# Seven-product FFN blocks: the first product copied by ScalarE into the bank in which its partner accumulates, and tails in another order

## The chip, the core and the metric

The kernel runs on one core of a Trainium2 chip. The metric is the device time of one execution in microseconds (us); less is better. Five engines work side by side, each through its own queue in order: TensorE (PE in the profile: matrix products and transposes, written to the banks of PSUM), VectorE (DVE), ScalarE (ACT), GpSimd (POOL) and SyncE (SP, which issues the weight loads). They wait for each other by semaphores.

## The reference

A decoder trunk of two layers on 256 tokens of width 1024, all in float32. Each layer is FFN, mixer, FFN, each with a layer norm behind it; the mixer is sparse attention in the first layer and a state-space scan (SSD) in the second. So there are four FFNs, and they are what the change touches:

```python
def swiglu_ffn(x, w_in, w_out):
    gate, up = jnp.split(x @ w_in, 2, axis=-1)
    return (jax.nn.silu(gate) * up) @ w_out

x = layer_norm(DEEPNORM_ALPHA * x + 0.5 * swiglu_ffn(x, ffn1_w_in[i], ffn1_w_out[i]), ln_g[i, 0], ln_b[i, 0])
```

with `D_FF = 2816`, that is 22 columns of 128 in the hidden layer.

## The kernel before

**Weights in two parts.** Every float32 weight tile (`raw`, 128 x 1024) is split into a high part `wh` (a cast by ScalarE, L321) and a low part `wl` (a subtraction by VectorE, L349), and every product is three matmuls: high by high, high by low, low by high (L528 to L530). `W.highs()` makes high parts ahead, `W.lows(keep)` makes the low parts that are still owed but for the last `keep`; `W.get(u)` makes what unit `u` still lacks. A raw tile is free for the next load when its last part is made.

**Order.** Nothing is scheduled by a tool. The instructions of every engine stand in the order in which the Python code issues them. In an FFN small pieces of work (GLUs, transposes) are put into `queue` by `later(f, d)`, to be issued `d` steps further on; each `step()` issues what is due (`items()`) and then makes weight parts (`W.pump`).

**An FFN** first does four hidden columns in the plain way (`wide`), two more singly (`one`), then 16 columns in four *seven-product blocks* (`seven`), in which two pairs of hidden columns (half-pairs `w` and `w + 1`) and the two token halves form a 2 x 2 block product with seven half products instead of eight. The sums of weights that it needs are made by VectorE (L288) or by accumulating DMAs that GpSimd issues (L261). Between the products stand pieces of the output product (`out()`, into the four `acc` banks). The last six output weights are the *tail*: token half 0 first, then half 1, with the layer norms of both halves.

In a block, `X` and `Y` are "pmm" banks, and `Z` is a "ptr" bank. The product A11 goes into X and is copied by ScalarE to SBUF (`p1`, L935), since X is needed for further sums. At the block's end A12 is made in Z, and VectorE adds: `nc.vector.tensor_add(p1, Z, p1)` (`c11`, L929). One step later comes the GLU on `p1`: SiLU by ScalarE (L773), then, a step later again, a multiplication by VectorE (L779).

When both token halves of a half-pair have their hidden values, `turn` transposes them on TensorE (L765) into a "ptr" bank; ScalarE casts the high part `hH` out of it (L766), and VectorE writes the low part `hL` (L767), which ends the use of the bank. This happens twice around a block's end: first for `w + 1` (tiles `c`, transposed ahead of the next block's first product) and then for `w` (tiles `c` and `h`, transposed behind the next block's second product). There are two "ptr" banks, handed out in turn.

**The tail** (`tail`) makes all the low parts that it can, then runs half 0, the layer norm of half 0 (L611 to L635), half 1, and, within half 1, the transposes of the new x of half 0 (`XT.fill(0)`, L546). The transposes of half 1 (`fill(1)`) come in the next stage.

Of the kernel before, what the change touches and what calls it, by code (L numbers as in the profile page):

```python
# [10 lines left out]
F32 = mybir.dt.float32  # L11
# [175 lines left out]
FILL = 2  # L187
# [220 lines left out]
def trunk_kernel(ctx: ExitStack, tc: tile.TileContext, widths, forms, x, ln_g, ln_b, wts, kvg, convp,  # L408
                 dt_bias, a_log, d_skip, norm_g, out):
    nc = tc.nc  # L410
# [37 lines left out]
    def pspare(n):  # L448
# [4 lines left out]
        a, b = divmod(spare[0] - 2, 2)  # L453
        return psum.tile([128, 512], F32, name=nm("psp"), tag=f"acc{a}{b}", bufs=1)

    def ptr():
        return psum.tile([128, 512], F32, name=nm("ptr"), tag="ptr", bufs=2)

    W = Weights(nc, f4, ring, wts, widths, forms, SLOTS, RAWS)

# [224 lines left out]
            c = slice(hf * 512, (hf + 1) * 512)  # L685
            mm3(acc[t][hf], lh, ll, H[:, c], L[:, c], first, last)

    def tail(acc, c, gb, ks, u, lhs, first, last, hook=None, early=0, ff=False):

        n = len(ks)
        nxt = None
        m = 0 if last else n - 3
        order = [[(i, hf) for a, b in ((0, n - 2), (n - 2, n)) for hf in range(2) for i in range(a, b)],
                 [(i, hf) for i in range(m) for hf in range(2)] + [(i, hf) for hf in range(2) for i in range(m, n)]]
        W.highs(8)
        W.lows()
        for t in range(2):
            for s, (i, hf) in enumerate(order[t]):  # L700
                if s == n and not t and hook:
                    hook()
                if s == n + FILL and t and not last:
                    nxt = XT(ff)
                    nxt.fill(0)
                H, L = W.get(u + i)
                if t and hf and last:
                    continue
                cs = slice(hf * 512, (hf + 1) * 512)
                mm3(acc[t][hf], *lhs(ks[i], t), H[:, cs], L[:, cs], first and i == 0, i == n - 1)  # L710
                if t and hf:
                    W.free(u + i)
                    if s < 2 * n - 2:
                        W.highs()
                        if s < n + FILL - early:
                            W.lows()
            rest = None
            if t and last:
                rest = pmm()[:, :256]
                for q, ps in enumerate((acc[t][1][:, :256], rest)):  # L720
                    ws = slice(512 + q * 256, 768 + q * 256)
                    for i, k in enumerate(ks):
                        H, L = W.get(u + i)
                        mm3(ps, *lhs(k, t), H[:, ws], L[:, ws], q == 1 and i == 0, i == n - 1)
            if t:
                W.lows(len(W.late) - 2)
            layernorm(t, acc[t], c, gb, last, rest, (lambda: W.lows(len(W.late) - 1)) if t and not last else None)
            if not t:
                W.highs(8)
                W.lows()  # L730
        return nxt

    def ffn(xT, u0, ln_i, first=False, last=False, ff=False):
# [9 lines left out]
        def later(f, d=1):  # L743

            while len(queue) < d:
                queue.append([])
            queue[d - 1].append(f)

        def items():
            for f in queue.pop(0) if queue else []:  # L750
# [18 lines left out]
        def glu(t, w, c, sil=None):  # L769


            g, h = (c[:, :256], c[:, 256:]) if sil is None else (sil, f1("h"))
            nc.scalar.activation(g, c[:, :256], AF.Silu)  # L773
            out_of = sil is not None and (w >= WIDE or (t and w and not first))
            if out_of:
                nc.scalar.copy(h, c[:, 256:])

            def mul():
                nc.vector.tensor_mul(h, h if out_of else c[:, 256:], g)  # L779
                W.owe(800)  # L780
                ready.setdefault(w, {})[t] = h
                if len(ready[w]) == 2:
                    later(lambda: later(turn(w, ready.pop(w))), 2)

            later(mul)

# [85 lines left out]
        def one(j):  # L872

            nonlocal u
            bank = pmm if j % 2 == 0 else ptr
            if j % 2 == 0:
                hH[j // 2], hL[j // 2] = r2("hH"), r2("hL")
            H, L = [a[j // 2][:, (j % 2) * 256:(j % 2 + 1) * 256] for a in (hH, hL)]
# [1 line left out]

            def half(o):
                nonlocal u
                ps = bank()
                proj_w(ps, xT, u)
                W.product()
                u += 1
# [16 lines left out]
        def seven(j, outs):  # L903
# [7 lines left out]
            w = j // 2  # L911
            for i in (w, w + 1):
                hH[i], hL[i] = r2("hH"), r2("hL")
            X, Y, Z = pmm(), pmm(), None
            c1, c2 = f4("c1"), f4("c2")
            p1, u2, u3, y5 = c1[:, :512], c1[:, 512:], c2[:, :512], c2[:, 512:]

            def c12():
                nc.vector.tensor_sub(u2, Y, u2)
# [5 lines left out]
                W.owe(600)  # L925
                later(lambda: glu(1, w + 1, y5))

            def c11():
                nc.vector.tensor_add(p1, Z, p1)  # L929
                W.owe(600)  # L930
                later(lambda: glu(0, w, p1))

            product(X, "A11", True)
            product(Y, "Q1", True)
            nc.scalar.copy(p1, X)  # L935
            nc.scalar.copy(y5, Y)
            step(4, most=-1)
            out()
# [8 lines left out]
            nc.scalar.copy(u3, X)  # L947
            later(c22)
            step(most=-1)
            Z = ptr()  # L950
            product(Z, "A12", True)
            later(c11)
            step(most=-1)
            out()
            product(X, "A22", False)
            glu(1, w, X, f1("sil"))
            step(most=-1)
            out()

        steps, ks = ffn_plan()  # L960
        for kind, j, outs in steps:
            W.raws = 9 if j < 18 else 7
            if kind == 'S':
                seven(j, outs)
            else:
                one(j)
                out_pieces(outs)
        while queue:
            items()
        gb = load_ln(ln_i)  # L970
        if first:
            load_consts()
        return u + len(ks), tail(acc, 0.5, gb, ks, u, lhs, False, last, ff=ff)

    def attention(xT, u, ln_i):
        kiT = f1("kiT")
# [771 lines left out]
```

## Time and profile before

| | |
|---|---|
| median of 3 runs | 1022.22 us (1021.9 to 1022.5) |
| profiled execution | 1022.91 us, span 1021.2 us |
| TensorE busy | 1003.4 us (98%), granted clock 0.999 |
| VectorE busy | 906.6 us (89%) |
| ScalarE busy | 660.9 us (65%) |
| GpSimd busy | 111.7 us (11%) |
| DMA | 231.70 MB, mean 227 GB/s |

The busy time of an engine is the time in which it executes an instruction; waiting is not in it. In rows of the timeline the first number is the start in us from the span's start, the second the duration of the (merged) instructions, then engine, line, operation, the tile written and those read, the shapes, the count, and in brackets the idle time of the engine ahead of it with what ended it. Instructions of one engine overlap a little: the next one starts somewhat before the end of the one ahead, so a queue's pace is read from start to start. A view of waits gives: who waited for whom, the sum in us, how many times, the longest.

### The profile page before, as it was taken

The page shows a single profiled execution, that of the slowest core. Times are in us where ns is not written, and L with a number is a line of the kernel's source. Part 1 is how long each engine was busy: PE and PEld are TensorE (multiplying, and loading weights), DVE is VectorE, ACT ScalarE, POOL GpSimd, SP SyncE. Part 2 cuts the span into 40 slices and gives each one's busy share as a digit, 9 for nine tenths or more (in the row PEclk, how much of TensorE's full clock was granted, in tenths as well). Part 3 has the DMA queues.
Part 4 walks back from the last instruction along what each step waited for, and adds up shares of the span by engine and source line. Part 5 has one row for each costly group of instructions (what it writes and reads, how often), then busy time and mean ns, then how long its engine had stood idle before and what let it go on. Part 6 is the DMA issues. An engine that isn't in the chain of part 4 may idle for free.

```text
span 1021.2 us, 14610 instructions
## 1 busy us (share of the span) xinstructions
PE 1003.4 (98%) x5279; PEld 848.4 (83%) x5279; DVE 906.6 (89%) x1264; ACT 660.9 (65%) x965; POOL 111.7 (11%) x161
## 2 busy tenths in 40 slices
PE   9999999999999999999999999999999999999996
PEld 7888888888788888887888888899898888888885
DVE  6899999789788999998899999788989978899996
ACT  6676876476655767764576775486876645676670
POOL 0010110100010101101010110150111101010101
PEclk9999999999999999999999999999999999999999
DMA  9699999452554899894499999467765654699971
GB/s 366 197 289 285 243 254 355 150 172 76 203 184 128 270 277 246 257 388 170 125 272 278 243 261 355 162 179 236 208 210 173 239 201 132 168 263 288 284 247 41
DMA packets 65336, 231.70 MB, mean 227 GB/s; under 512 B 8032, under 2 KB 8032, under 8 KB 65264
## 3 DMA queue, kind: packets, MB, share of 16 engines
q1 hardware_dynamic: 53856, 189.84, 50.8%
q0 software_dynamic: 11120, 40.41, 21.6%
q8 instruction: 41, 0.67, 0.3%
q10 hardware_dynamic: 288, 0.52, 0.1%
q14 instruction: 31, 0.25, 0.1%
HBM read 193.48 MB, written 1.08 MB: 191 GB/s over the span
## 4 chain that ended last, share of the span: by engine, by line
PE 86%; DVE 8%; DMA 3%; issue 1%; ACT 1%; POOL 1%; POOLq 0%; DVEq 0%
PE pmm L530 13%; PE pmm L528 13%; PE pmm L529 13%; PE acc L528 8%; PE acc L530 8%; PE acc L529 8%; DVE wl L349 3%; PE ptr L530 2%; PE ptr L529 2%; PE ptr L528 2%; PE pxs L528 2%; PE pxs L530 2%; PE pxs L529 2%; PE pmm L677 1%; PE ptr L677 1%; DMA raw<-in_wts_dram 1%
## 5 line engine op out<-in xcount | busy, mean ns | idle before, releaser
L349 DVE TENSOR_TENSOR wl<-raw,wh 128x1024 fp32r<-128x1024 f32 (+2 forms) x423 | 494.8, 1213 | 14.1 <-ACT wh L321 13.9
L321 ACT CAST wh<-raw 128x1024 fp32r<-128x1024 f32 (+3 forms) x430 | 428.1, 1044 | 90.8 <-DVE raw L288 48.7
L529 PE MATMUL acc<-wl,hH 128*128 128x512 f32 (+1 forms) x352 | 136.8, 389 | 1.6 <-DVE wl L349 1.6
L528 PE MATMUL acc<-wh,hH 128*128 128x512 f32 (+1 forms) x352 | 138.1, 392 | 0.0
L530 PE MATMUL acc<-wh,hL 128*128 128x512 f32 (+1 forms) x352 | 136.6, 388 | 0.0
L528 PE MATMUL pmm<-wh,xT 128*128 128x512 f32 (+2 forms) x320 | 126.0, 394 | 0.0
L530 PE MATMUL pmm<-wh,xT 128*128 128x512 f32 (+2 forms) x320 | 123.4, 386 | 0.4 <-DVE xT L525 0.2
L529 PE MATMUL pmm<-wl,xT 128*128 128x512 f32 (+2 forms) x320 | 122.8, 384 | 0.0
L261 POOL DMA_DIRECT2D raw<-raw x64 | 55.7, 876 | 489.4 <-DVE raw L288 256.6
L530 PE MATMUL pmm<-wh,xf 128*128 128x512 f32 x256 | 99.6, 389 | 0.0
L528 PE MATMUL pmm<-wh,xf 128*128 128x512 f32 x256 | 99.6, 389 | 0.0
L529 PE MATMUL pmm<-wl,xf 128*128 128x512 f32 x256 | 99.6, 389 | 0.0
L529 PEld LDWEIGHTS acc<-wl,hH 128*128 128x128 f32 x352 | 66.2, 188 | 16.2 <-DVE wl L349 3.3
L530 PEld LDWEIGHTS acc<-wh,hL 128*128 128x128 f32 x352 | 66.1, 188 | 13.5
L288 DVE TENSOR_TENSOR raw<-raw,raw 128x1024 f32<-128x1024 f32 x64 | 77.0, 1218 | 0.2
L528 PEld LDWEIGHTS acc<-wh,hH 128*128 128x128 f32 x352 | 66.1, 188 | 13.0
L530 PEld LDWEIGHTS pmm<-wh,xT 128*128 128x128 f32 x320 | 60.1, 188 | 13.8 <-DVE xT L525 1.7
L529 PEld LDWEIGHTS pmm<-wl,xT 128*128 128x128 f32 x320 | 60.4, 189 | 10.9 <-DVE wl L349 0.3
L528 PEld LDWEIGHTS pmm<-wh,xT 128*128 128x128 f32 x320 | 60.3, 188 | 10.5
L528 PEld LDWEIGHTS pmm<-wh,xf 128*128 128x128 f32 x256 | 48.0, 188 | 10.0
L529 PEld LDWEIGHTS pmm<-wl,xf 128*128 128x128 f32 x256 | 48.0, 188 | 10.0
L530 PEld LDWEIGHTS pmm<-wh,xf 128*128 128x128 f32 x256 | 48.0, 188 | 9.9
(307 smaller groups left out, 1768.4 us busy)
## 6 DMA issues: line engine op xcount, KB each, us to landing
raw<-in_wts_dram SPq DMA_DIRECT2D x339, 512.0 KB, 5.9
raw<-raw POOLq DMA_DIRECT2D x64, 512.0 KB, 5.5
M<-scr POOLq DMA_DIRECT2D x8, 512.0 KB, 5.9
lng<-in_ln_g_dram SPq DMA_DIRECT2D x6, 512.0 KB, 5.3
lnb<-in_ln_b_dram SPq DMA_DIRECT2D x6, 512.0 KB, 5.9
wl<-raw POOLq DMA_DIRECT2D x5, 512.0 KB, 5.5
raw<-in_wts_dram SPq DMA_DIRECT2D x4, 408.0 KB, 5.0
out_dram<-x SPq DMA_DIRECT2D x4, 256.0 KB, 2.0
```

The source lines that it names most:

```text
L261: self.nc.gpsimd.dma_start(self.raw[r], self.raw[other], accum_op=ALU.add)
L288: self.nc.vector.tensor_add(self.raw[r], self.raw[r], self.raw[other])
L321: nc.scalar.copy(h[:, c:c + n], raw[:, c:c + n])
L349: self.nc.vector.tensor_sub(lo[:, s], raw[:, s], h[:, s].bitcast(F32))
L528: nc.tensor.matmul(ps, lh, rh, start=first, stop=False, skip_group_check=on)
L529: nc.tensor.matmul(ps, lh, rl, start=False, stop=False, skip_group_check=on)
L530: nc.tensor.matmul(ps, ll, rh, start=False, stop=last, skip_group_check=on)
L677: nc.tensor.matmul(ps, H[:, k * 128:(k + 1) * 128], xT.HL[:, k, :], start=k == 0, stop=False)
```

## The change

1. In a block, `Z` is taken at the start, and ScalarE copies A11 into it (`nc.scalar.copy(Z, X)`) instead of into SBUF. A12 is then accumulated onto it by TensorE (its first matmul no longer clears the bank). VectorE's addition `c11` is gone, and the GLU is issued at once behind A12, reading from the bank: SiLU and a copy of the second half by ScalarE, and the multiplication by VectorE at the next step.
2. `ptr()` names its two banks: they are handed out in turn, but as long as a block holds one for `Z`, every other call gets the other one. Both transposes around a block's end fall into that time.
3. `turn`'s second part (hL) is put ahead of what is queued for the next step (`soon`), instead of behind it.
4. In the tails of the FFNs (`own=True`), up to two low parts that belong to the next stage are left for later; those made within half 1 too; and one low part is made ahead of the last `items()`.

```diff
+    bank, held = [0], [None]
+
     def ptr():
-        return psum.tile([128, 512], F32, name=nm("ptr"), tag="ptr", bufs=2)
+        bank[0] = 1 - bank[0] if held[0] is None else 1 - held[0]
+        return psum.tile([128, 512], F32, name=nm("ptr"), tag=f"ptr{bank[0]}", bufs=1)
...
         W.highs(8)
-        W.lows()
+        W.lows(min(2, sum(v >= u + n for v in W.late)) if own else 0)
...
                     nxt.fill(0)
+                    if own:
+                        W.lows(1)
...
-                        if s < n + FILL - early:
+                        if s < n + FILL - early and not own:
                             W.lows()
...
+        def soon(f):
+            if not queue:
+                queue.append([])
+            queue[0].insert(0, f)
...
-                    later(lambda: later(turn(w, ready.pop(w))), 2)
+                    later(lambda: soon(turn(w, ready.pop(w))), 2)
...
-            X, Y, Z = pmm(), pmm(), None
+            X, Y, Z = pmm(), pmm(), ptr()
+            held[0] = bank[0]
...
-            def c11():
-                nc.vector.tensor_add(p1, Z, p1)
-                W.owe(600)
-                later(lambda: glu(0, w, p1))
-
             product(X, "A11", True)
             product(Y, "Q1", True)
-            nc.scalar.copy(p1, X)
+            nc.scalar.copy(Z, X)
...
-            Z = ptr()
-            product(Z, "A12", True)
-            later(c11)
+            product(Z, "A12", False)
+            glu(0, w, Z, f1("sil"))
             step(most=-1)
             out()
             product(X, "A22", False)
             glu(1, w, X, f1("sil"))
             step(most=-1)
             out()
+            held[0] = None
...
+        W.lows(1)
         while queue:
             items()
...
-        return u + len(ks), tail(acc, 0.5, gb, ks, u, lhs, False, last, ff=ff)
+        return u + len(ks), tail(acc, 0.5, gb, ks, u, lhs, False, last, ff=ff, own=True)
```

How instructions move: TensorE's are the same ones in the same order. On VectorE, at the end of the second block of the second FFN, before (`c_472` is the tile of `p1`, `c_473` that of `y5`, `ptr_3793` is Z, `raw` in L288 are sums of weights):

```order
L349 TENSOR_TENSOR wl_3767<-raw_3415,wh_3766 128x1024
L929 TENSOR_TENSOR c_472_3623<-ptr_3793,c_472_3623 128x512
L349 TENSOR_TENSOR wl_3788<-raw_3436,wh_3787 128x1024
L349 TENSOR_TENSOR wl_3791<-raw_3691,wh_3790 128x1024
L779 TENSOR_TENSOR c_473_3624<-c_473_3624 128x256
L349 TENSOR_TENSOR wl_3815<-raw_3693,wh_3814 128x1024
L349 TENSOR_TENSOR wl_3818<-raw_3713,wh_3817 128x1024
L288 TENSOR_TENSOR raw_3693<-raw_3693,raw_3737 128x1024
L288 TENSOR_TENSOR raw_3713<-raw_3713,raw_3739 128x1024
L779 TENSOR_TENSOR c_472_3623<-c_472_3623 128x256
L779 TENSOR_TENSOR h_3856<-h_3856,sil_3855 128x256
```

And after (all lines of the program's later part are numbered some 3 to 10 higher; L789 is the multiplication, `h_3817` and `sil_3816` are the GLU of Z):

```order
L349 TENSOR_TENSOR wl_3778<-raw_3424,wh_3777 128x1024
L789 TENSOR_TENSOR h_3817<-h_3817,sil_3816 128x256
L349 TENSOR_TENSOR wl_3799<-raw_3445,wh_3798 128x1024
L349 TENSOR_TENSOR wl_3802<-raw_3702,wh_3801 128x1024
L789 TENSOR_TENSOR c_484_3635<-c_484_3635 128x256
L349 TENSOR_TENSOR wl_3829<-raw_3704,wh_3828 128x1024
L349 TENSOR_TENSOR wl_3832<-raw_3724,wh_3831 128x1024
L288 TENSOR_TENSOR raw_3704<-raw_3704,raw_3748 128x1024
L288 TENSOR_TENSOR raw_3724<-raw_3724,raw_3750 128x1024
L789 TENSOR_TENSOR h_3869<-h_3869,sil_3868 128x256
```

The addition is gone, and the multiplication that stood behind both L288 now stands where the addition was. On ScalarE at the same place, before:

```order
L947 COPY c_473_3624<-pmm_3621 128x512
L321 CAST wh_3787<-raw_3436 128x1024
L321 CAST wh_3790<-raw_3691 128x1024
L773 ACTIVATE c_473_3624<-c_473_3624 128x256
L321 CAST wh_3814<-raw_3693 128x1024
L321 CAST wh_3817<-raw_3713 128x1024
L773 ACTIVATE c_472_3623<-c_472_3623 128x256
```

And after:

```order
L953 COPY c_484_3635<-pmm_3631 128x512
L321 CAST wh_3798<-raw_3445 128x1024
L321 CAST wh_3801<-raw_3702 128x1024
L783 ACTIVATE sil_3816<-ptr_3633 128x256
L786 COPY h_3817<-ptr_3633 128x256
L783 ACTIVATE c_484_3635<-c_484_3635 128x256
L321 CAST wh_3828<-raw_3704 128x1024
L321 CAST wh_3831<-raw_3724 128x1024
```

The SiLU of this half moved ahead by two casts, and a copy out of the bank came with it. On VectorE in the tail of the second FFN, from the last multiplication to the layer norm of half 0, before:

```order
L779 TENSOR_TENSOR h_4406<-h_4406,sil_4405 128x256
L349 TENSOR_TENSOR wl_4391<-raw_4312,wh_4390 128x1024
L767 TENSOR_TENSOR hL_4174<-ptr_4432,hH_4173 128x512
L767 TENSOR_TENSOR hL_4172<-ptr_4438,hH_4171 128x512
L349 TENSOR_TENSOR wl_4415<-raw_4314,wh_4414 128x1024
L349 TENSOR_TENSOR wl_4418<-raw_4335,wh_4417 128x1024
L349 TENSOR_TENSOR wl_4451<-raw_4360,wh_4450 128x1024
L349 TENSOR_TENSOR wl_4454<-raw_4362,wh_4453 128x1024
L349 TENSOR_TENSOR wl_4457<-raw_4386,wh_4456 128x1024
L349 TENSOR_TENSOR wl_4460<-raw_4388,wh_4459 128x1024
L349 TENSOR_TENSOR wl_4463<-raw_4412,wh_4462 128x1024
L611 SCALAR_TENSOR_TENSOR x_71<-acc_3392,x_71 128x512
```

And after:

```order
L789 TENSOR_TENSOR h_4423<-h_4423,sil_4422 128x256
L349 TENSOR_TENSOR wl_4408<-raw_4327,wh_4407 128x1024
L349 TENSOR_TENSOR wl_4431<-raw_4329,wh_4430 128x1024
L777 TENSOR_TENSOR hL_4188<-ptr_4451,hH_4187 128x512
L777 TENSOR_TENSOR hL_4186<-ptr_4458,hH_4185 128x512
L349 TENSOR_TENSOR wl_4434<-raw_4350,wh_4433 128x1024
L349 TENSOR_TENSOR wl_4470<-raw_4378,wh_4469 128x1024
L349 TENSOR_TENSOR wl_4473<-raw_4380,wh_4472 128x1024
L349 TENSOR_TENSOR wl_4476<-raw_4403,wh_4475 128x1024
L614 SCALAR_TENSOR_TENSOR x_71<-acc_3401,x_71 128x512
```

One low part moved ahead of the two hL, and two of the seven behind them now stand behind the layer norm of half 0 (ahead of the transposed x's low parts).

More of the change, by code (lines that the diff above doesn't have):

```diff
@@ L686, in out_k, with tail @@
             mm3(acc[t][hf], lh, ll, H[:, c], L[:, c], first, last)
-    def tail(acc, c, gb, ks, u, lhs, first, last, hook=None, early=0, ff=False):
+    def tail(acc, c, gb, ks, u, lhs, first, last, hook=None, early=0, ff=False, own=False):
         n = len(ks)
@@ L874, in one @@
             nonlocal u
-            bank = pmm if j % 2 == 0 else ptr
+            half_bank = pmm if j % 2 == 0 else ptr
             if j % 2 == 0:
@@ L882, in half @@
                 nonlocal u
-                ps = bank()
+                ps = half_bank()
                 proj_w(ps, xT, u)
@@ L913, in seven @@
                 hH[i], hL[i] = r2("hH"), r2("hL")
-            X, Y, Z = pmm(), pmm(), None
+            X, Y, Z = pmm(), pmm(), ptr()
+            held[0] = bank[0]
             c1, c2 = f4("c1"), f4("c2")
-            p1, u2, u3, y5 = c1[:, :512], c1[:, 512:], c2[:, :512], c2[:, 512:]
+            u2, u3, y5 = c1[:, 512:], c2[:, :512], c2[:, 512:]
             def c12():
```

## Prediction

> **What bounds the kernel now.** I read the page first: the busy times, then the chain that ended last.
>
> ```profile
> PE 1003.4 (98%) x5279; PEld 848.4 (83%) x5279; DVE 906.6 (89%) x1264; ACT 660.9 (65%) x965; POOL 111.7 (11%) x161
> PE 86%; DVE 8%; DMA 3%; issue 1%; ACT 1%; POOL 1%; POOLq 0%; DVEq 0%
> ```
>
> TensorE is busy for 1003.4 of 1021.2 us and is 86% of the chain. VectorE is off the path but has little room of its own: 89% over the whole span. The change leaves TensorE's instructions and their order as they are, so all it can do is add or take away waits of TensorE. The view of waits, for TensorE, shows those that VectorE causes:
>
> ```profile
> PE acc L529 <- DVE wl L349: 1.6, 4, 0.4
> PE pxT L546 <- DVE x L635: 1.3, 3, 0.8
> PE ptr L546 <- DVE x L635: 1.1, 2, 0.8
> PE pmm L530 <- DVE xT L525: 0.2, 1, 0.2
> ```
>
> Columns: sum in us, times, longest. Nearly all of these 4.2 us lie in the FFN tails (the last six output weights, then the layer norm of half 0). No row names a transpose L765 or a product of a seven-product block: inside the blocks TensorE waits for nothing. So at most about 4 us can be won, and only in the tails; in the blocks there are only waits to be added.
>
> **The removed addition, and what stands in its place.** This is VectorE, then ScalarE, then TensorE in the timeline, around the end of the second block of the second FFN and the start of its third block:
>
> ```profile
> 375.50 1.22 DVE L349 TENSOR_TENSOR wl<-raw,wh 128x1024 fp32r<-128x1024 f32 x1
> 376.95 0.69 DVE L929 TENSOR_TENSOR c<-ptr,c 128x512 f32<-128x512 f32 x1 [0.23 <-PE ptr L530]
> 377.56 2.35 DVE L349 TENSOR_TENSOR wl<-raw,wh 128x1024 fp32r<-128x1024 f32 x2
> ...
> 382.44 2.35 DVE L288 TENSOR_TENSOR raw<-raw,raw 128x1024 f32<-128x1024 f32 x2
> 384.71 0.42 DVE L779 TENSOR_TENSOR c<-c 128x256 f32<-128x256 f32 x1
> 385.37 0.43 DVE L779 TENSOR_TENSOR h<-h,sil 128x256 f32<-128x256 f32 x1 [0.24 <-ACT h L776]
> 385.71 3.49 DVE L349 TENSOR_TENSOR wl<-raw,wh 128x1024 fp32r<-128x1024 f32 x3
> 389.12 1.22 DVE L288 TENSOR_TENSOR raw<-raw,raw 128x1024 f32<-128x1024 f32 x1
> 390.26 0.68 DVE L767 TENSOR_TENSOR hL<-ptr,hH 128x512 fp32r<-128x512 f32 x1
> ```
>
> ```profile
> 374.23 0.59 ACT L947 COPY c<-pmm 128x512 f32<-128x512 f32 x1 [1.70 <-PE pmm L530]
> 375.83 2.00 ACT L321 CAST wh<-raw 128x1024 fp32r<-128x1024 f32 x2 [1.01 <-DMA raw<-raw]
> 377.74 0.41 ACT L773 ACTIVATE c<-c 128x256 f32<-128x256 f32 x1
> 383.74 1.06 ACT L321 CAST wh<-raw 128x1024 fp32r<-128x1024 f32 x1 [3.39 <-DVE raw L288]
> 384.70 0.37 ACT L773 ACTIVATE sil<-pmm 128x256 f32<-128x256 f32 x1
> 384.98 0.36 ACT L776 COPY h<-pmm 128x256 f32<-128x256 f32 x1
> 391.05 0.59 ACT L936 COPY c<-pmm 128x512 f32<-128x512 f32 x1 [1.90 <-PE pmm L530]
> ```
>
> ```profile
> 390.62 0.39 PE L530 MATMUL pmm<-wh,xf 128*128 128x512 f32 x1
> 390.85 0.38 PE L765 MATMUL ptr<-ident,c 128*128 128x128 f32 x2
> ```
>
> Before, VectorE waits 0.23 us for the product A12 and adds (0.61 us from start to next start). After, its next instruction there is the GLU's multiplication, which needs a SiLU and a copy by ScalarE out of the bank, and these stand in ScalarE's queue behind two weight casts. The second cast of a block's last sum waits for a DMA accumulation (idle 1.01 here, "DMA raw<-raw"). So after: SiLU at 377.74 (where the old SiLU started); multiplication 0.67 later, as from 384.70 to 385.37, at 378.41; VectorE free 0.34 later (385.37 to 385.71), at 378.75. Before it was free at 377.56. VectorE is late by d = 1.19 us, though it has one instruction less. In general d is ScalarE's idle time before that cast plus 0.18, and not less than 0.40, since SiLU, copy and multiplication (0.67 + 0.34) take the place of an addition of 0.61 even where ScalarE waits only for the product.
>
> Does VectorE catch up? The multiplication that no longer stands at 384.71 saves 0.34, but the next one waits for ScalarE (0.24 idle), whose cast at 383.74 waits for the first L288. That chain moves by d as a whole. From 385.71 VectorE has no gap up to the write of hL at 390.26, so hL ends at 390.94 + d.
>
> **The bank.** Who needs that hL in time? Before, the two transposes of a block's ends (first of half-pair w+1, then of w) use the two "ptr" banks in turn, and nobody waits. After, Z holds one bank from the block's start to its end, and both transposes share the other: the second, at 390.85 in TensorE's order, must wait until VectorE has read the first, that is until hL is written. Before, the transpose starts 0.09 us ahead of that end. A release by VectorE takes 0.06 to TensorE (below: L635 ends at 461.57 + 0.75 = 462.32, transpose at 462.38). So TensorE waits d + 0.15, at three boundaries in each of four FFNs, 12 in all. (The fourth block's transposes fall behind the last block, where the banks are no longer held.) The shares of the idle time over all blocks:
>
> ```profile
> ACT wh L321 <- DMA raw<-raw: 11.5, 16, 1.3
> DVE c L919 <- ACT c L942: 13.5, 16, 1.1
> ```
>
> The first row gives 11.5 / 16 = 0.72 us a block, so d is 0.90 on average (1.48 at most, 0.40 at least). The second says that VectorE waits some 0.8 us for TensorE at L919 in every block: there the two fall into step again, so the delay doesn't pile up; but as TensorE was delayed 0.15 more than VectorE, the DMA accumulations of the next block start 0.15 early, and only the first boundary of each FFN pays the 0.15. Sum: 12 x 0.90 + 4 x 0.15 = 11.4 us. Bounds: 12 x 0.55 = 6.6 (every d at its least) and 12 x 1.63 = 19.6 (every d at its most).
>
> **Smaller parts of the blocks.** ScalarE's copy of the first product now goes into a bank; no row shows ScalarE writing a bank. The nearest row is the copy into SBUF beside it (0.59 at 391.05); as 1.90 us of idle follow before that one, waiting for TensorE, anything from nothing to 2.4 us for it is hidden, and I take nothing. The 16 extra ScalarE instructions (0.25 us each) fall into gaps of 1 to 3 us. The multiplication at 384.71 changes its place only.
>
> **The tails.** Here VectorE gets one low part ahead of the two hL (into the idle time behind the last multiplication) and two behind the layer norm of half 0 instead of ahead of it. From the second FFN's tail:
>
> ```profile
> 457.08 0.68 DVE L611 SCALAR_TENSOR_TENSOR x<-acc,x 128x512 f32<-128x512 f32 x1
> 461.57 0.75 DVE L635 SCALAR_TENSOR_TENSOR x<-x,rs,lnb 128x512 f32<-128x512 f32 x1 [0.73 <-POOL rs L520]
> 463.69 3.49 DVE L349 TENSOR_TENSOR wl<-raw,wh 128x1024 fp32r<-128x1024 f32 x3
> 469.43 0.68 DVE L611 SCALAR_TENSOR_TENSOR x<-acc,x 128x512 f32<-128x512 f32 x1
> 475.36 0.75 DVE L635 SCALAR_TENSOR_TENSOR x<-x,rs,lnb 128x512 f32<-128x512 f32 x1
> ```
>
> ```profile
> 462.38 0.66 PE L546 MATMUL pxT<-ident,x 128*128 128x128 f32 x4 [0.34 <-DVE x L635]
> 463.83 0.66 PE L546 MATMUL pxT<-ident,x 128*128 128x128 f32 x4 [0.79 <-DVE x L635]
> 476.36 1.03 PE L546 MATMUL pxT<-ident,x 128*128 128x128 f32 x8
> ```
>
> Three low parts of 1.14 us (3.49 / 3) leave the stretch ahead of 457.08, so the layer norm of half 0 can start up to 3.4 us earlier, as soon as its accumulator is done. The four waits of acc L529 (1.6 us) and those for half 0 go away. What is late next: the layer norm of half 1. Two low parts more stand ahead of it (2.3 us), so it starts at about 469.2 instead of 469.43, and its x is done at 475.36 + 0.75 = 476.1, where the second four of the transposes at 476.36 (at about 476.8) need it. TensorE can come only 0.7 + 0.2 = 0.9 us earlier there, not the 1.7 that its waits give. Likewise 0.7 in the first FFN; 0.7 in the third and 0.4 in the last, where the waits themselves are the limit. Together 2.7 us; between 1.6 (the waits for wl alone) and 4.2.
>
> **Sum.** 1022.9 us (the profiled execution, 1.7 above its span) + 11.4 - 2.7 = 1031.6. The median of the runs before lies 0.7 below the profiled one, so I forecast 1030.9 us, slower by 0.8%. About 0.2% (2 us) is what a measurement of this kernel can tell from no change.
>
> **The rivals.**
> 1. Tails and additions decide: hL comes in time. For it: hL was written only 0.09 us after the transpose starts. It takes a d below about 0.08 at every boundary (12 x (d + 0.15) less than 2.7), which means that ScalarE finishes SiLU and copy by the time at which the old addition ended. Against it: 0.67 + 0.34 stand against 0.61 even with no DMA wait. Time: 1022.2 - 2.7 = 1019.5, with all of the tails' waits 1018.0. Chance 0.06.
> 2. VectorE's instructions are on the path after all, and each addition taken away is time won: 16 x 0.61 = 9.8 us, so 1012.4. Against it: TensorE waits for VectorE 4.2 us in all, and none of it at the additions. Chance 0.01. The Trainium skill speaks for this one: "VectorE: DVE Perf Modes", section Rules for kernel authors, advises to cut the number of VectorE instructions. By that rule the count alone would tell; the trace agrees that an instruction of 512 columns costs 0.61 us of VectorE, and disagrees that VectorE sets the end.
> 3. About even: every d at its least (the accumulations land earlier because TensorE leaves them more time) and the tails win all: 1022.2 + 6.6 - 4.2 = 1024.6, or somewhat better, since a first boundary needs no more than 0.55. Within 0.2%: 0.08; between that and 1027 is part of my own case.
> 4. The lateness feeds itself: the accumulations that ScalarE waits for are issued by GpSimd after VectorE's low parts, so if their landing moves by more than the delay (they share the rings with twelve weight loads a block), d goes to its most: 1022.2 + 19.6 - 2.7 = 1039. Against it: they fall into step at L919. Chance 0.10.
> 5. My forecast, 1026 to 1035: 0.75.
>
> So faster 0.07, same 0.08, slower 0.85. The range 1022.5 to 1036.0 takes in most of 3 and the lower part of what lies between 5 and 4.
>
> **What would show it.** Right: a new row of TensorE's waits, ptr L775 on hL L777, 12 times, about 1 us each; VectorE's multiplication L789 at the block's end idle 1 to 2 us ahead of it, for ScalarE; the addition gone; the acc L532 waits gone; waits at L549 fewer but not gone (half 1 late). Wrong: no such row, or d below 0.3 because the weight casts stand earlier than I read, or waits for low parts (acc or pmm L532 on wl) in the blocks' middle, which would mean that VectorE's delay is not taken up at L919.

## The result, and the profile after

| | before | after |
|---|---|---|
| median | 1022.06 us (4 runs, 1021.61 to 1022.50) | 1029.99 us (4 runs, 1029.21 to 1030.94) |
| profiled execution, span | 1022.91 us, 1021.2 us | 1029.21 us, 1027.4 us |
| TensorE, VectorE busy | 1003.4, 906.6 us | 1005.1, 897.7 us |

The change makes the kernel slower: ratio 1.0074, 95% interval 1.0061 to 1.0086. Ratios and intervals, here and below, leave out four slow executions (1247, 2541 and 2835 us in two of the experiments, 1681 us of the kernel before), which the medians take in. VectorE has 8.9 us less to do, and the end comes 7.9 us later. TensorE's waits for VectorE in the profile after (sum in us, times, longest):

```profile
PE ptr L775 <- DVE hL L777: 5.9, 12, 1.0
PE ptr L549 <- DVE x L638: 2.2, 3, 0.9
PE pxT L549 <- DVE x L638: 1.7, 3, 0.8
PE pmm L532 <- DVE wl L349: 0.2, 1, 0.2
```

The first row is new, and it has the 12 waits of the forecast, at 0.5 us each where about 1 was forecast. The four waits of acc for wl are gone; those for x are still there, three and three instead of three and two. One of the 12 places, the end of the second block of the second FFN (the place of the prediction's rows), is this in VectorE's, ScalarE's and TensorE's timeline after:

```profile
378.97 1.22 DVE L349 TENSOR_TENSOR wl<-raw,wh 128x1024 fp32r<-128x1024 f32 x1
381.11 0.42 DVE L789 TENSOR_TENSOR h<-h,sil 128x256 f32<-128x256 f32 x1 [0.92 <-ACT h L786]
381.45 2.35 DVE L349 TENSOR_TENSOR wl<-raw,wh 128x1024 fp32r<-128x1024 f32 x2
...
389.26 0.43 DVE L789 TENSOR_TENSOR h<-h,sil 128x256 f32<-128x256 f32 x1 [0.58 <-ACT h L786]
389.60 3.49 DVE L349 TENSOR_TENSOR wl<-raw,wh 128x1024 fp32r<-128x1024 f32 x3
393.01 1.22 DVE L288 TENSOR_TENSOR raw<-raw,raw 128x1024 f32<-128x1024 f32 x1
394.15 0.69 DVE L777 TENSOR_TENSOR hL<-ptr,hH 128x512 fp32r<-128x512 f32 x1
```

```profile
377.71 0.59 ACT L953 COPY c<-pmm 128x512 f32<-128x512 f32 x1 [1.69 <-PE pmm L533]
378.19 2.00 ACT L321 CAST wh<-raw 128x1024 fp32r<-128x1024 f32 x2
380.43 0.38 ACT L783 ACTIVATE sil<-ptr 128x256 f32<-128x256 f32 x1 [0.23 <-PE ptr L533]
380.71 0.37 ACT L786 COPY h<-ptr 128x256 f32<-128x256 f32 x1
```

```profile
388.39 0.60 PE L775 MATMUL ptr<-ident,c 128*128 128x128 f32 x4
...
394.07 0.39 PE L533 MATMUL pmm<-wh,xf 128*128 128x512 f32 x1
394.89 0.66 PE L775 MATMUL ptr<-ident,h 128*128 128x128 f32 x4 [0.43 <-DVE hL L777]
```

The reader sees the chain of the forecast: VectorE waits 0.92 for ScalarE (1 to 2 were forecast) where it had waited 0.23 for TensorE; from 389.26 on it runs without a gap; hL ends at 394.15 + 0.69 = 394.84, and the second transpose starts 0.05 later. Only one thing differs from the forecast: ScalarE's two casts follow the copy at once. The wait of 1.01 us for the accumulating DMA, which stood there before, is gone.

**Where the time went.** TensorE's instructions are the same in all kernels of this study, so the start of each can be compared with its start before, and the difference cut by stages. Three sums are worked out in that way: *blocks* (the four stretches with seven-product blocks), *tails* (the four tails with the start of what follows), and *d*, the mean over the 12 boundaries of how much later hL starts, counted from the first transposes (5.34 us before).

| kernel | blocks | tails | d | median, us |
|---|---|---|---|---|
| after | +8.5 | -2.1 | 0.50 | 1029.99 |
| tails only | 0.0 | -2.1 | | 1019.88 |
| blocks only | +8.4 | -0.1 | 0.49 | 1031.08 |
| bank held only | +2.5 | 0.0 | 0.00 | 1025.54 |
| multiplication three steps on | 0.0 | -2.1 | -0.93 | 1019.83 |
| addition behind | +15.9 | -2.1 | 1.11 | 1035.84 |
| addition ahead | +19.7 | | 1.43 | 1041.26 |
| addition ahead, other operand | +8.4 | | 0.48 | 1029.48 |
| bank Y | +8.0 | -2.2 | 1.14 | 1028.76 |
| bank Y, tile of another ring | +4.6 | -2.1 | 0.84 | 1024.84 |
| buffer held longer | +9.0 | -2.1 | 0.53 | 1028.95 |
| buffer taken earlier | +12.0 | -2.1 | 0.79 | 1031.96 |
| three steps on, low part moved | 0.0 | -3.5 | | 1019.21 |

(Where the tails have no number, a slow spell of TensorE's clock fell into the first of them; see the last section. The two kernels with the multiplication three steps on have the same d.) Wherever both transposes share a bank and d is not negative, *blocks* is 12 x (d + 0.21) within 0.2 us. Two more pieces stand in every comparison with the profiled execution of before: that one had 1.5 us in the state-space scan which all others have not, or have in part only (its row "acc <- DVE xtok", 0.9 us, among others), and the first 12 us of the kernel took from 0.2 us less to 1.5 us more. I put neither down to the change: the kernels with the tails only and with the bank held only, which have none of each other's edits, lack the piece of the scan too, and the piece at the start goes mostly with TensorE's clock (last section). For the changed kernel the pieces make 8.5 - 2.1 - 1.5 + 1.4 = 6.3, which is the difference of the two profiled executions.

### The profile page after: what moved, and what is told of

Its sections match the earlier page's. It is cut to its first block, busy times and chain, and to the rows that moved or that the text cites. A ratio compares the mean times of both kernels' runs of the same rounds, so it can differ in the third digit from the quotient of the medians.

```text
span 1027.4 us, 14570 instructions
## 1 busy us (share of the span) xinstructions
PE 1005.1 (98%) x5279; PEld 849.0 (83%) x5279; DVE 897.7 (87%) x1248; ACT 665.7 (65%) x981; POOL 111.5 (11%) x161
## 4 chain that ended last, share of the span: by engine, by line
PE 67%; DVE 17%; issue 8%; ACT 3%; DMA 3%; POOL 2%; DVEq 0%; POOLq 0%; ACTq 0%
PE pmm L531 8%; PE pmm L532 8%; PE pmm L533 8%; DVE wl L349 8%; PE acc L531 6%; PE acc L533 6%; PE acc L532 6%; DVE raw L288 3%; DMA raw<-raw 3%; ACT wh L321 2%; PE ptr L533 2%; PE ptr L531 2%; PE ptr L532 2%; PE pxs L531 2%; PE pxs L533 1%
## 5 line engine op out<-in xcount | busy, mean ns | idle before, releaser
L532 PE MATMUL acc<-wl,hH 128*128 128x512 f32 (+1 forms) x352 | 136.4, 387 | 0.0
L532 PE MATMUL pmm<-wl,xT 128*128 128x512 f32 (+2 forms) x320 | 123.5, 386 | 0.2 <-DVE wl L349 0.2
L532 PE MATMUL pmm<-wl,xf 128*128 128x512 f32 x256 | 99.6, 389 | 0.0
L288 DVE TENSOR_TENSOR raw<-raw,raw 128x1024 f32<-128x1024 f32 x64 | 77.1, 1220 | 0.2
L532 PEld LDWEIGHTS acc<-wl,hH 128*128 128x128 f32 x352 | 66.2, 188 | 13.0
L532 PEld LDWEIGHTS pmm<-wl,xT 128*128 128x128 f32 x320 | 60.6, 190 | 11.5 <-DVE wl L349 0.8
L532 PEld LDWEIGHTS pmm<-wl,xf 128*128 128x128 f32 x256 | 48.1, 188 | 10.0
```

The source lines that it names most:

```text
L288: self.nc.vector.tensor_add(self.raw[r], self.raw[r], self.raw[other])
L532: nc.tensor.matmul(ps, lh, rl, start=False, stop=False, skip_group_check=on)
```

## The experiments

All were timed in five rounds beside the kernel before, whose median was 1022.0 to 1022.1 us each time.

### The tails alone

```diff
+        W.lows(1)
         while queue:
             items()
...
-        return u + len(ks), tail(acc, 0.5, gb, ks, u, lhs, False, last, ff=ff)
+        return u + len(ks), tail(acc, 0.5, gb, ks, u, lhs, False, last, ff=ff, own=True)
```

(with `own` in `tail` as in the change; blocks as before)

> The kernel before with part 4 of the change alone (the tails; blocks, banks and hL as before). Theory: half 0's layer norm comes earlier, half 1's comes later, and the two nearly cancel; adding up TensorE's waits in the tails of the two profiles gives -1.0 us, so 1021.1 us, with rows of waits L549 <- x L638 for half 1. The prediction's own sum for the tails: -2.7, so 1019.4 us. Rival: the tails cost, since half 1's layer norm ends later than before: 1022.5 or more.

Measured: 1019.88 us, ratio 0.9981 (0.9972 to 0.9989). The tails are a gain of 2.1 us, between the theory (1.0) and the prediction's sum (2.7). The theory had added up only the differences of over 0.2 us in TensorE's starts; the smaller ones that it had left out are worth another 1.1.

### The blocks alone

The changed kernel without `own=True` and without the last `W.lows(1)`.

> The changed kernel with the tails of before (parts 1 to 3 of the change without part 4). Theory: all of the loss is in the blocks, 12 waits of TensorE for hL of 0.56 to 1.2 us, about 7.9 in sum: 1022.1 + 7.9 = 1030.0 us, and not less than the changed kernel. Rival: a part of the loss comes from the tails (VectorE late there, low parts missing at the start of the next stage): then 1028 us or less.

Measured: 1031.08 us, ratio 1.0090 (1.0076 to 1.0105). All of the loss is in the blocks, 9.1 us by the medians, 8.4 by the starts.

### The bank held, and nothing else

```diff
-            X, Y, Z = pmm(), pmm(), None
+            X, Y, Z = pmm(), pmm(), ptr()
+            held[0] = bank[0]
...
-            Z = ptr()
             product(Z, "A12", True)
             later(c11)
...
+            held[0] = None
```

(on the kernel before, with `ptr` and `soon` of the change)

> The kernel before with the bank held and nothing else of the blocks: Z is taken at the block's start and kept to its end, so that both transposes share the other bank, and hL is put ahead of what is queued (without that the second transpose would be issued ahead of the hL that frees its bank). The addition and the copy to SBUF stay, and VectorE's work is that of before. Theory: the loss needs both the shared bank and the late hL; with hL as early as before, TensorE lacks 0.15 us at each of 12 boundaries: 1022.1 + 1.8 = 1023.9 us at most, 1022.7 if only the first boundary of each FFN pays. Rival: the shared bank alone costs nearly all of it (a pair of transposes that can't overlap with the reading of the first): 1028 to 1030 us.

Measured: 1025.54 us, ratio 1.0033 (1.0021 to 1.0045). From the same place, VectorE and TensorE:

```profile
392.61 0.68 DVE L775 TENSOR_TENSOR hL<-ptr,hH 128x512 fp32r<-128x512 f32 x1
```

```profile
392.94 0.39 PE L533 MATMUL pmm<-wh,xf 128*128 128x512 f32 x1
393.35 0.44 PE L773 MATMUL ptr<-ident,c 128*128 128x128 f32 x2
```

hL comes as early as before (d = 0.00 at all 12 boundaries), and the transpose starts 0.06 behind its end. The shared bank alone costs 2.5 us by the starts (3.5 by the medians): 0.21 at each of the 12 boundaries (0.15 were expected), and all 12 pay it, not the first of each FFN only. It is not the main part.

### The multiplication three steps on

```diff
-        def glu(t, w, c, sil=None):
+        def glu(t, w, c, sil=None, d=1):
...
-            later(mul)
+            later(mul, d)
...
-            glu(0, w, Z, f1("sil"))
+            glu(0, w, Z, f1("sil"), 3)
```

> The changed kernel with one number changed: the multiplication of the GLU on Z is issued three steps further on (where it stood before the change) instead of one; the SiLU and the copy out of the bank stay early. Bank sharing and tails as in the changed kernel. Theory: VectorE no longer waits for ScalarE where the addition was, it saves the addition, and hL ends 0.6 to 0.8 us earlier than before the change: no waits for hL at the second transposes, 1022.1 - 1.0 (tails) = 1021.1 us. Rival (the bank alone): the waits stay, 1028 to 1030 us. Rival (the addition's 0.61 us counts for TensorE): 16 x 0.61 less than before, about 1012 us.

Measured: 1019.83 us, ratio 0.9981 (0.9972 to 0.9989), the time of the tails alone. VectorE at the same place:

```profile
381.27 2.35 DVE L288 TENSOR_TENSOR raw<-raw,raw 128x1024 f32<-128x1024 f32 x2
383.55 0.42 DVE L789 TENSOR_TENSOR h<-h,sil 128x256 f32<-128x256 f32 x1
384.21 0.42 DVE L789 TENSOR_TENSOR h<-h,sil 128x256 f32<-128x256 f32 x1 [0.24 <-ACT h L786]
...
389.09 0.69 DVE L777 TENSOR_TENSOR hL<-ptr,hH 128x512 fp32r<-128x512 f32 x1
```

The multiplication on Z stands at 383.55, without a wait; hL comes 0.93 us earlier than before the change, and no row L775 <- hL is left among TensorE's waits. Addition gone, copy into the bank, bank shared: none of it costs anything if the multiplication stands where ScalarE is done. It gains nothing either: 16 additions fewer on VectorE leave the blocks at 0.0.

### One addition more on VectorE, behind and ahead of the multiplication

```diff
             glu(0, w, Z, f1("sil"))
+            later(lambda: nc.vector.tensor_add(c1[:, :512], u3, y5))
```

> The changed kernel with a VectorE addition of the old size (128 x 512, on two SBUF tiles, its sum read by nobody) put right behind the multiplication of the GLU on Z. Theory: VectorE runs without a gap from there to hL but for one wait for ScalarE that moves along with it, so hL comes 0.6 us later and TensorE pays it at all 12 boundaries: 1030.0 + 7.2 = 1037.2 us. Rival: the 0.6 us of idle time ahead of the last multiplication takes it up: 1030 us.

Measured: 1035.84 us, ratio 1.0135 (1.0119 to 1.0150). By the starts the blocks cost 7.4 us more than in the changed kernel (5.9 by the medians), 0.61 at each boundary, just the duration from start to start of such an addition. TensorE's row grows from 5.9 to

```profile
PE ptr L775 <- DVE hL L777: 12.8, 12, 1.2
```

The same line ahead of `glu`:

> The same extra VectorE addition, put right ahead of the multiplication of the GLU on Z instead of behind it. Theory: VectorE waits there some 0.9 us for ScalarE anyway, so the addition falls into that wait and costs nothing: 1030.0 us. Rival (a VectorE instruction costs its time wherever it stands): as with the one behind, about 1037 us.

Measured: 1041.26 us, ratio 1.0186 (1.0172 to 1.0200). The expectation failed, by its operand:

```profile
385.45 0.69 DVE L957 TENSOR_TENSOR c<-c 128x512 f32<-128x512 f32 x1 [1.24 <-ACT c L783]
386.06 0.42 DVE L789 TENSOR_TENSOR h<-h,sil 128x256 f32<-128x256 f32 x1
```

The addition read y5, and ScalarE makes the SiLU of y5 behind its copy out of the bank; so VectorE waited 1.24 for that third instruction and only then added. With `u3, u3` as operands:

> The extra VectorE addition ahead of the multiplication of the GLU on Z once more, reading only u3, on which ScalarE has no more work (in the run before it read y5 too, whose SiLU stands behind ScalarE's copy out of the bank, so VectorE waited for that as well). Theory: it falls into VectorE's wait of 0.9 us for ScalarE, at no cost beyond some tenths at boundaries where that wait is shorter: but as it writes the half p1 it can't start a block late; 1030 us, with d as in the changed kernel. Rival (an instruction costs its time wherever it stands): 1037 us.

Measured: 1029.48 us, ratio 1.0069 (1.0057 to 1.0081), against 1029.99 without it.

```profile
380.97 0.69 DVE L957 TENSOR_TENSOR c<-c 128x512 f32<-128x512 f32 x1
382.32 0.42 DVE L789 TENSOR_TENSOR h<-h,sil 128x256 f32<-128x256 f32 x1 [0.66 <-ACT h L786]
```

It falls into the wait. The same addition (but for one operand) costs 7.4 us in the blocks behind the multiplication and nothing ahead of it: what counts is not how many instructions VectorE has, but whether they stand between ScalarE's result and hL.

### A bank for each transpose

```diff
-            X, Y, Z = pmm(), pmm(), ptr()
-            held[0] = bank[0]
+            X, Y = pmm(), pmm()
...
-            nc.scalar.copy(Z, X)
+            nc.scalar.copy(p1, X)
...
             out()
+            nc.scalar.copy(Y, p1)
             product(X, "S3", False)
...
-            product(Z, "A12", False)
-            glu(0, w, Z, f1("sil"))
+            product(Y, "A12", False)
+            glu(0, w, Y, f1("sil"))
```

> The changed kernel with another bank for the copy: the product A11 is copied to SBUF as before, and then by a second ScalarE copy into the bank Y, once VectorE has read Y; A12 is accumulated there. No ptr bank is held, so the two transposes of a boundary have a bank each. The addition is gone, the multiplication stands one step on as in the changed kernel, VectorE is as late, the tails are the changed ones. Theory: nobody waits for hL, the blocks lose nothing, 1019.9 us as with the multiplication three steps on. Rival (VectorE's lateness reaches TensorE by another way, low parts or products): 1023 us or more.

Measured: 1028.76 us, ratio 1.0063 (1.0051 to 1.0076). The theory fell. The row for hL is gone, and another has come, with ScalarE's wait for the accumulating DMA longer than before the change (11.5 us, 16 times):

```profile
PE pmm L532 <- DVE wl L349: 3.7, 11, 0.4
...
ACT wh L321 <- DMA raw<-raw: 14.8, 14, 1.7
```

VectorE is later here (d = 1.14), and its lateness reaches TensorE through low parts: by the starts, the products that wait for them hold some 7.4 of the 8.0 us. With `p1` in a tile of another ring (`p1 = f2("p1")`; why, see the next part):

> As the kernel with the copy into bank Y (a bank for each transpose, addition gone, multiplication one step on), but A11's copy in SBUF lies in a tile of another ring, so c1 is taken as late as in the changed kernel. Theory: the loss of 6.6 us in the first form came from the buffer taken early (accumulations late, VectorE over 1 us late, low parts late); with d back at some 0.5 and no bank shared, TensorE waits neither for hL nor for low parts in the blocks: 1020 us, as with the multiplication three steps on. Rival: low parts are late anyway, 1024 us or more.

Measured: 1024.84 us, ratio 1.0029 (1.0016 to 1.0042). Better by 3.9 us, but not without loss:

```profile
PE pmm L532 <- DVE wl L349: 2.0, 6, 0.4
...
ACT wh L321 <- DMA raw<-raw: 11.0, 12, 1.2
...
DVE c L930 <- ACT c L948: 8.2, 16, 1.1
```

The first boundary of each FFN has d = 0.42, the later ones 0.77 to 1.32: VectorE doesn't fall into step again. Its wait at L930 (L919 before) was 13.5 us before the change and 16.2 in the changed kernel; here it is 8.2. As I read it, in the changed kernel TensorE's own wait for hL is what lets VectorE catch up; no run here tries that by itself, and both kernels with bank Y also have one ScalarE copy more in each block, whose part no run separates. What is shown is that the lateness costs TensorE time with the shared bank and without it; I had taken the shared bank to be needed for that.

### Why d was 0.50 and not 0.90

ScalarE's wait for the accumulating DMA was 11.5 us before (16 times) and is 2.8 in the changed kernel. The ring of tiles that holds the raw weights also holds a block's `c1` and `c2`. First attempt: `c1` was free later before the change, since the second transposes read its half `p1`. A tiny VectorE copy of `c1` behind hL of half-pair w + 1 keeps it (`hold[w + 1] = c1`):

```diff
+                if w in hold:
+                    c = hold.pop(w)
+                    nc.vector.tensor_copy(c[:, :8], c[:, 512:520])
```

> The changed kernel with one tiny VectorE copy (128 x 8) of the block's tile c1 behind the first hL of a boundary. It keeps c1's buffer, which comes from the same ring of twelve as the raw weight tiles, as long as before the change (then the half p1 of that tile was read by the second transposes); after the change c1 is free at the first transposes, some 6 us earlier. Theory: the early release lets one weight load per block start earlier, so that it no longer runs beside the accumulating transfer for which ScalarE waits; with the buffer held ScalarE's idle time for that transfer goes from 2.8 us (7 times) back to about 11 us (16 times), d from 0.5 to 0.9, and the time to 1030.0 + 12 x 0.4 = 1034.8 us. Rival (the transfers are quicker because TensorE's waits give them time): row and time as in the changed kernel, 1030 to 1031 us.

Measured: 1028.95 us, ratio 1.0066 (1.0054 to 1.0079); ScalarE's row is 4.1 us, 6 times. This theory fell. The other end of the tile's life: before, its first write was the copy of A11 at the block's start; after, it is the copy of S2. So take the buffer early again:

```diff
             nc.scalar.copy(Z, X)
+            nc.scalar.copy(c1[:, :8], X[:, :8])
```

> The changed kernel with one tiny ScalarE copy (128 x 8) into the block's tile c1, where before the change the copy of A11 into p1 (a half of that tile) stood. It takes c1's buffer of the ring of twelve (which the raw weight tiles share) at the block's start, as before the change; after the change the first write of c1 is the copy of S2, about a third of a block later, and until then the ring has one buffer more for weights. New theory (that of the early release fell): with the buffer taken early, three weight loads per block wait for one low part more, one of them runs beside the accumulating transfer again, ScalarE's idle time for that transfer goes from 2.8 us (7 times) back to 11 us or more (16 times), d from 0.50 to 0.9 or 1.0, and the time to 1030.0 + 12 x (0.4 to 0.5) = 1035 to 1036 us. Rival (loads don't set it): 1029 to 1030 us.

Measured: 1031.96 us, ratio 1.0099 (1.0086 to 1.0112): 2.0 us more than the changed kernel by the medians, 3.5 by the starts of the blocks. Less than expected, in the direction expected. ScalarE's wait in the changed kernel, and with the buffer taken early:

```profile
ACT wh L321 <- DMA raw<-raw: 2.8, 7, 0.8
```

```profile
ACT wh L321 <- DMA raw<-raw: 8.4, 13, 1.3
```

Worked out from the issues and landings of the four accumulating transfers of a block: the last one took 8.90 us on average before, 8.28 after, 8.29 with the multiplication three steps on, and 8.88 with the buffer taken early (8.87 with the bank held only, where `p1` is still in `c1`). So one tiny write of 8 columns takes the gain away. Counted in the same way, 4 weight loads are issued between the issue of that transfer and its landing in every block before and with the buffer taken early, and 3 in most blocks of the changed kernel (3.25 on average). That the load which runs beside it is what slows the transfer is my reading.

The buffer is not all of it. With the bank held only, where the buffer is taken as before, ScalarE's wait is shorter than before, too:

```profile
ACT wh L321 <- DMA raw<-raw: 8.1, 13, 1.4
```

That is 3.4 us less than 11.5, or 0.21 a block. TensorE loses just as much there at each boundary, while VectorE, behind whose low parts the accumulations are issued, loses nothing; as I read it, they so land that much earlier as TensorE counts. With the buffer taken early the changed kernel has 8.4, about the same; the rest of the way, from 8.4 to 2.8, goes with the buffer. And the late buffer alone doesn't do it: with bank Y and a tile of another ring the last transfer is as short as in the changed kernel (8.37), but TensorE doesn't wait for hL, and ScalarE waits 11.0 us, 12 times; with the multiplication three steps on, where VectorE is early, it waits 0.7 us in all.

### One more low part moved in the tails

```diff
                     if own:
-                        W.lows(1)
+                        W.lows(2)
```

(on the kernel with the multiplication three steps on)

> The kernel with the multiplication three steps on (1019.8 us), and in the tails one low part more left for later (two instead of one behind the transposes of half 0's x): it goes from ahead of half 1's layer norm into VectorE's wait for GpSimd's root (0.72 us). Theory: half 1's x comes 1.14 - 0.42 = 0.7 us earlier, TensorE's waits for it shrink by 0.7 in each of three tails: 1019.8 - 2.1 = 1017.7 us. Rival: the moved low part comes too late for the next stage's product, and TensorE waits for it as long: 1019.8 us or more.

Measured: 1019.21 us, ratio 0.9969 (0.9958 to 0.9981), the lowest median of all, 2.8 us below the kernel before; its interval overlaps that of the multiplication three steps on (1019.83 us). By the starts the tails win 1.4 us more, 0.45 in each of three, where 0.7 were expected:

```profile
471.18 1.18 DVE L349 TENSOR_TENSOR wl<-raw,wh 128x1024 fp32r<-128x1024 f32 x1
472.28 0.74 DVE L634 SCALAR_TENSOR_TENSOR x<-x,mv,lng 128x512 f32<-128x512 f32 x1
473.46 0.75 DVE L638 SCALAR_TENSOR_TENSOR x<-x,rs,lnb 128x512 f32<-128x512 f32 x1 [0.44 <-POOL rs L523]
```

The low part stands in the wait as meant, and yet 0.44 of waiting is left: GpSimd's two instructions of the root take 0.70 longer (last section). Of the low part's 1.14 that leaves the 0.44 won.

## Why the prediction was right, and where it was off

**TensorE's instructions unchanged, only waits can come or go:** right. **VectorE late by the multiplication that waits for ScalarE:** right, and it is the cause: with the multiplication three steps on the loss is 0.0, and an instruction behind it costs its full 0.61 at each boundary.

**The size of d:** this is the term that was mis-sized. Forecast 0.90 on average with a floor of 0.40; measured 0.50, at eight of the twelve boundaries 0.40 to 0.42. The floor was exact. What failed is the reading that ScalarE's wait for the accumulation (11.5 us, 16 times) would stay: it fell to 2.8 us, 7 times. Most of that (5.6 us) goes with `c1`'s buffer, which the change also takes later; the prediction didn't look at it. The rest (3.1 us) is near the 3.4 that the shared bank alone takes off; the prediction named an early start of the accumulations, but kept d at the old wait. With the buffer taken early d is 0.79 and the blocks lose 12.0 us, near the 11.4 of the sum.

**The bank:** TensorE loses d + 0.21, not d + 0.15, and at each boundary; 0.06 more for a pair of transposes that waits. That only the first boundary of an FFN pays the 0.15 was wrong (12 x 0.21 = 2.5 with the bank held alone). The two errors work against each other: 12 x (0.50 + 0.21) = 8.5 against 11.4.

**VectorE and TensorE in step again at L919:** true of the changed kernel, where TensorE waits; not true in the kernel with bank Y and a tile of another ring, where it doesn't. (The row of L919 names a copy by ScalarE, not TensorE as the prediction says; that copy itself waits for a product.)

**Copy into the bank hidden:** right; the blocks stand at 0.0 in the kernel with the multiplication three steps on, which has it.

**The tails:** forecast -2.7, measured -2.1. By FFN it was 0.5, 0.7, 0.1 and 0.75 where 0.7, 0.9, 0.7 and 0.4 were forecast, so the third was much overrated and the last underrated. The acc waits went (0.57 each by the starts), the x waits of half 0 too, and half 1's layer norm is late next, as said. A new wait of 0.2 for a low part (pmm L532 on wl) lies behind the third tail, not in a block's middle.

**The sum:** 1030.9 forecast (1022.5 to 1036.0), 1029.99 measured. Of the terms 8.5 - 2.1 = 6.4 is shown; the medians differ by 7.9. The runs of the changed kernel scatter over 1.7 us, and the profiled one is the fastest of the four; the remaining 1.5 us I can't place. A slow spell of TensorE's clock, as in the last section, would be of that size, but the mean clocks of the four executions (0.996 and 0.997) don't settle it. That the forecast came within 0.9 us is in part luck: its terms add up to 8.7, those shown by the starts to 6.4, and the 1.5 us without a place fill most of the gap.

**The rivals.** The count of VectorE's instructions (rival 2) is refuted by the pair of additions above: the same count, 7.5 us apart in the blocks. The Trainium skill's advice to cut it ("VectorE: DVE Perf Modes", Rules for kernel authors) would not have helped here; by the trace 16 additions fewer are worth nothing. "hL in time" (rival 1) didn't happen, but it can be made to. Rival 3 had the mechanism that occurred, accumulations that land earlier: its own reason, that TensorE leaves them more time, fits the kernel with the bank held only (0.21 a block less to wait), and the later buffer, which it didn't name, is the larger part. Rival 4, lateness that feeds itself, was wrong with the shared bank and is seen in a small way without it.

## What to carry to other kernels

An instruction taken from an engine is worth nothing, or less, if what stands in its place waits for another engine's queue: look at what stands between that wait and the next thing that the bound engine needs, and move the waiter behind work that is ready. When a buffer's use changes, its first write and its last read both move, and with a shared ring that shifts transfers that seem to have nothing to do with the edit. A wait that a busy engine shows may be what keeps the others in step; when it is taken away the lateness can come out elsewhere.

## What the hardware showed that was not expected

**GpSimd beside VectorE.** GpSimd's two instructions of the root, in the kernel with the multiplication three steps on, where VectorE runs its L634 beside the first and waits beside the second; and with the low part moved, where it runs the low part beside the first and L634 beside the second:

```profile
472.06 0.75 POOL L521 TENSOR_SCALAR rse<-mv 128x1 f32<-128x1 f32 x1 [13.22 <-DVE mv L627]
472.89 0.55 POOL L523 TENSOR_TENSOR rs<-rse,mhalf 128x1 f32<-128x1 f32 x1
```

```profile
471.35 1.06 POOL L521 TENSOR_SCALAR rse<-mv 128x1 f32<-128x1 f32 x1 [12.10 <-DVE mv L627]
472.49 0.94 POOL L523 TENSOR_TENSOR rs<-rse,mhalf 128x1 f32<-128x1 f32 x1
```

They take 2.00 instead of 1.30 us, on one column; the second alone takes 0.94 beside L634 and 0.55 with VectorE idle. The Trainium skill ("GPSIMD Engine Reference", Specifications) says that the two engines share their interfaces to SBUF and contend when a VectorE instruction has two SBUF inputs; the low part and L634 have two, and these rows agree.

**TensorE's clock.** Matmuls of one shape start 0.43 us apart in the first microseconds and 0.23 later. In the profiled execution of before and in that of after, with the same instructions:

```profile
8.07 0.39 PE L530 MATMUL pmm<-wh,xT 128*128 128x512 f32 x1
8.30 0.39 PE L528 MATMUL pmm<-wh,xT 128*128 128x512 f32 x1
```

```profile
8.18 0.63 PE L533 MATMUL pmm<-wh,xT 128*128 128x512 f32 x1
8.61 0.63 PE L531 MATMUL pmm<-wh,xT 128*128 128x512 f32 x1
```

The full pace sets in at 8.07 in the one and at 11.10 in the other, which makes the 1.4 us at the start. Over all profiles here it set in between 7.9 and 11.2, and the first 12 us of the kernels differ by up to 1.7 us. The view by stretches gives a granted clock of 1.00 in both, so that column doesn't show it; the pace does. The same came back in the middle of two profiles, both with an addition ahead: behind the two waits of 0.89 and 0.82 us for half 1's x in the first tail, matmuls of 512 columns again started 0.43 us apart in the kernel with the other operand, and its granted clock was 0.55 in the stretch from 198 to 201 us (view by stretches: length, busy time and count of TensorE, its weight loads, VectorE, ScalarE and GpSimd, then granted clock, DMA share and GB/s):

```profile
198.00:201.00 3.00, 3.00 (x13) 2.90 (x12) 1.16 (x4) 0.59 (x2) 0.00 (x0) 0.55 0.65 259
```

against 1.00 in the changed kernel behind the same two waits (0.88 and 0.82); it cost 1.5 us. The Trainium skill ("TensorE: Matmul & The Clock Gate", Part 1) says that the clock is set by activity in a window that runs freely, and that the point of the change so varies by half a microsecond either way. That it varies agrees, but here it does so by over 3 us; the window itself no run shows.

**ScalarE into a bank.** The copy of 512 columns into a bank takes 594 ns on average. The copy of the same product into SBUF took 596 before, and the copy that follows it takes 586 (groups by line, of after, after and before: busy us, mean ns, then the idle time ahead of them):

```profile
L941 ACT COPY ptr<-pmm 128x512 f32<-128x512 f32 x16 | 9.5, 594 | 3.2 <-PE pmm L533 3.2
L942 ACT COPY c<-pmm 128x512 f32<-128x512 f32 x16 | 9.4, 586 | 25.2 <-PE pmm L533 25.2
...
L935 ACT COPY c<-pmm 128x512 f32<-128x512 f32 x16 | 9.5, 596 | 3.0 <-PE pmm L530 3.0
```

The Trainium skill ("ScalarE: Activation LUTs", Step-by-step: what each stage is for) calls the bank the quicker destination; here the two differ by 10 ns at most, either way.
